# A decoder trunk layer in split float32 on one core: splits of the first projection in another order, operand sums and reloads elsewhere, square sums by single-column products

## The chip, the cores and the metric

The kernel runs on one core of a Trainium2 chip. The metric is the device time of one execution in microseconds. Three executions of the kernel before took 1136.26, 1137.62 and 1137.86 us (median 1137.62).

## The reference

One layer of a decoder trunk over 512 tokens of width 1024, all in float32:

```python
h = rms_norm(x, norm_mix)
rq, rk, rv, rg, cq, ckv, krope, gr, gm = split(h @ w_in)
ro = rms_norm(retention(rope(rq), rope(rk) * 256**-0.5, rv))        # 4 heads, 256 / 512 wide
a_ret = (ro * silu(rg)) @ w_br
q = rms_norm(rms_norm(cq) @ w_uq)                                   # 8 heads, 128 + 64 (rotary)
k_nope, v = split(rms_norm(ckv) @ w_ukv);  k = rms_norm([k_nope, krope])
a_mla = causal_attention(rope(q), rope(k), v) @ w_bm
x = x + (sigmoid(gr) * a_ret + sigmoid(gm) * a_mla) @ w_o
x = x + relu(rms_norm(x) @ w_up)**2 @ w_down                        # 4096 wide
x = x + sigmoid(rms_norm(x) @ w_ple_gate) * (p @ w_ple)
```

The norms of q and k in the attention need, for each head and token, the sum of squares over the 128 non-rotary channels (and the rotary ones): these are the square sums of this text.

## The kernel before

Activations lie with channels on the 128 partitions and the 512 tokens along the free axis, in [128, 512] tiles. Every float32 operand of a product is split into a high part of the matmul's reduced type and the remainder, and each product is three matmuls (`mm3`, line 168 in the profile: low times high, high times low, high times high), so nearly all TensorE work is matmuls of 512 columns. ScalarE writes the high part (`wh_...` of a weight chunk at line 261, `...h` of an activation in `split`), VectorE the rest (`wl_...` at line 263 or 265, `...l`). A product can start only when both are there.

The program is a list of steps (`step(key, function, arguments)`), run in order. A step with a weight key has its chunk of at most [128, 1024] fetched by SyncE's queue (`wr_...`) into one of six raw tiles and split one chunk ahead, into one of three pairs of split tiles, so a split of a chunk waits until TensorE is done with the chunk three earlier. TensorE's instructions keep the order of the list. Those of ScalarE, VectorE and POOL, and the transfers, are ordered by a scheduler where the code does not pin them (`keep_in_program_order`), and each engine then works its instructions off strictly in that order: one that waits holds all behind it.

Tiles of the working pool (`T`, 45 of them) and of a second pool for longer-lived operands (`K`, 16) are reused in turn; PSUM has eight banks (`B`).

The stages, with the names in the profile: the first projection `pA` (key-value latent; eight row chunks `a1`, operands `xg0` to `xg7` = x times a gain, 72 matmuls), the query latent `pcq`, the attention gates `gm` and the heads (`pk`, `pq`, `pv`, scores `sc`, transposes `pt`, output `mo`), with token statistics by matmuls against a column of ones (`stx`, `stkv`; each as two records of 128x1), then the attention branch `bm` with its gates `gb` reloaded from DRAM (`zm..d`), then four retention heads: `rq`, `rk`, the values `rv` for two heads at a time and the gate `rg`, both by Strassen-like products numbered 1, 7, 2, 6, 5, 4, 3 on sums of operand blocks (`x_operand`: s7, s6, s5, s3, each two tiles `..0` and `..1` with parts h and l), the masked scores `rs` (split into `ath` and `atl`, four blocks s.0 to s.3), the output `ro`, and the branch `br`. For the products 6 and 4 the weight blocks are summed in DRAM transfers that accumulate into the raw tile, issued by POOL. Branch sums and gates wait in DRAM and are reloaded (`re`, `ze`, `ge`, for the branch sum, the attention share and the retention gate), mixed (`mix`), and go through the output projection `wo`; then come the MLP (`up`, `dn`) and the gated embedding (`pg`).

The square sums of two heads (a pair) are formed in two steps: `pair_sums` sums squares with a [128, 32] block of ones, four products of 512 columns on four column groups of the array at once, ScalarE copies the result, and `pair_stats` turns four 128-token blocks with transposes (`st`), from which VectorE works out the head factors (`ha`, `hr`); these are broadcast (`pbk`) for the scores.

Before the first products, seven matmuls on a zeroed tile (`zero`) are issued. In the head of the program, three chunks and three operands are split in the order of the code's loop, the rest inside `first_products`.

## Time and profile before

| | |
|---|---|
| median of three executions | 1137.62 us (1136.26 to 1137.86) |
| the profiled execution | 1134.75 us |
| its span on the engines | 1133.0 us |
| mean granted TensorE clock | 0.993 |
| TensorE busy | 1108.0 us (98%), 5547 matmuls and as many weight loads |
| VectorE, ScalarE, POOL busy | 735.5, 537.1, 85.5 us |
| transfers | 175.97 MB, 155 GB/s over the span |

A row of a profile's list names line, engine, operation and output<-inputs, with buffer numbers left out (`wl_rk<-wr_rk,wh_rk`), then the count and times. The list of waits names the engine that stood, what it waited for, the sum, how often, and the longest. In the chain of waits each row is a stretch of the chain that ended last: start, length, what. A window row gives busy time with instruction counts for TensorE, its weight loads, VectorE, ScalarE and POOL, then the granted clock, the DMA share and GB/s.

### The profile page before, as it was taken

What the parts mean: (1) busy time and instruction counts of PE and PEld (TensorE: products, weight loads), DVE (VectorE), ACT (ScalarE), POOL (GpSimd) and SP (SyncE); (2) the same over time, 40 slices, a digit from 0 to 9 for tenths busy, and PEclk for the clock granted to TensorE, in tenths of its full rate; (3) what the DMA queues carried; (4) which work ended last, traced back from release to release, by engine and by line L of the source; (5) the groups of instructions that cost most, each with busy time, mean ns of one, the idle gap of its engine ahead of it and who ended that gap; (6) DMA issues with size and microseconds to landing.
All of it is one profiled execution on the core that took longest, in us unless ns stands there. A gap on an engine that the chain in (4) does not pass through costs nothing.

```text
span 1133.0 us, 14696 instructions
## 1 busy us (share of the span) xinstructions
PE 1108.0 (98%) x5547; PEld 938.7 (83%) x5547; DVE 735.5 (65%) x1206; ACT 537.1 (47%) x762; POOL 85.5 (8%) x113
## 2 busy tenths in 40 slices
PE   8999999999899999999999999999999999999998
PEld 6887878888689989888988977888888888888877
DVE  5787687565766755845684668646566566668675
ACT  6556656443354545444543543434444443445542
POOL 0000000001111011022003000010100100101000
PEclk8999999999899999999999999999999999999999
DMA  7223231356498265479638473694745855737511
GB/s 230 77 89 127 61 103 49 120 206 213 139 205 215 94 207 139 130 172 237 184 115 190 131 288 121 198 265 141 155 158 178 176 162 159 184 130 205 150 37 74
DMA packets 59223, 175.97 MB, mean 155 GB/s; under 512 B 7248, under 2 KB 8656, under 8 KB 58896
## 3 DMA queue, kind: packets, MB, share of 16 engines
q1 hardware_dynamic: 45168, 129.66, 33.6%
q0 software_dynamic: 13840, 45.36, 20.7%
q8 instruction: 43, 0.70, 0.2%
q14 instruction: 28, 0.23, 0.1%
q10 hardware_dynamic: 144, 0.03, 0.0%
HBM read 156.92 MB, written 15.99 MB: 153 GB/s over the span
## 4 chain that ended last, share of the span: by engine, by line
PE 90%; DVE 5%; DMA 2%; ACT 2%; issue 2%; SPq 0%; DVEq 0%; ACTq 0%
PE up L168 15%; PE dn L168 13%; PE rg L168 7%; PE rv L168 7%; PE br L168 6%; PE rk L168 4%; PE pg L168 4%; PE wo L168 3%; PE gr L168 3%; PE bm L168 3%; PE rq L168 3%; PE gm L168 3%; PE ro L168 3%; PE sc L168 2%; PE pA L168 2%
## 5 line engine op out<-in xcount | busy, mean ns | idle before, releaser
L168 PE MATMUL dn<-wh_dn,cl 128*128 128x512 f32 x224 | 87.2, 389 | 0.0
L168 PE MATMUL dn<-wh_dn,ch 128*128 128x512 f32 x224 | 87.2, 389 | 0.0
L168 PE MATMUL dn<-wl_dn,ch 128*128 128x512 f32 x224 | 87.1, 389 | 0.0
L261 ACT ACTIVATE wh_dn<-wr_dn 128x1024 fp32r<-128x1024 f32 x32 | 34.0, 1063 | 75.4 <-PE up L168 54.3
L261 ACT ACTIVATE wh_up<-wr_up 128x1024 fp32r<-128x1024 f32 x32 | 34.0, 1061 | 57.4 <-PE up L168 29.3
L263 DVE TENSOR_TENSOR wl_dn<-wr_dn,wh_dn 128x1024 fp32r<-128x1024 f32 x32 | 39.1, 1220 | 27.5 <-ACT wh_dn L261 27.5
L263 DVE TENSOR_TENSOR wl_up<-wr_up,wh_up 128x1024 fp32r<-128x1024 f32 x32 | 39.1, 1222 | 17.7 <-ACT wh_up L261 17.7
L263 DVE TENSOR_TENSOR wl_rg<-wr_rg,wh_rg 128x1024 fp32r<-128x1024 f32 x20 | 24.4, 1222 | 38.5 <-ACT wh_rg L261 38.3
L168 PEld LDWEIGHTS dn<-wh_dn,ch 128*128 128x128 f32 x224 | 42.0, 188 | 8.8
L168 PEld LDWEIGHTS dn<-wh_dn,cl 128*128 128x128 f32 x224 | 42.0, 188 | 8.8
L951 DVE SCALAR_TENSOR_TENSOR f<-up,bcx 128x512 f32<-128x512 f32 x32 | 20.6, 685 | 44.1 <-PE up L168 44.1
L168 PEld LDWEIGHTS dn<-wl_dn,ch 128*128 128x128 f32 x224 | 42.0, 188 | 8.6
L261 ACT ACTIVATE wh_dn<-dr_dn 128x1024 fp32r<-128x1024 f32 x24 | 25.5, 1060 | 42.2 <-PE up L168 29.1
L223 POOL DMA_DIRECT2D dr_dn<-wstream x24 | 21.4, 896 | 312.1 <-DVE rx L326 119.6
L263 DVE TENSOR_TENSOR wl_dn<-dr_dn,wh_dn 128x1024 fp32r<-128x1024 f32 x24 | 29.3, 1222 | 22.4 <-ACT wh_dn L261 22.4
L261 ACT ACTIVATE wh_rv<-wr_rv 128x1024 fp32r<-128x1024 f32 x28 | 29.6, 1059 | 28.5 <-PE rv L168 12.0
L261 ACT ACTIVATE wh_rg<-wr_rg 128x1024 fp32r<-128x1024 f32 x28 | 29.6, 1056 | 25.2 <-DMA wr_rg<-wstream 17.0
L263 DVE TENSOR_TENSOR wl_br<-wr_br,wh_br 128x1024 fp32r<-128x1024 f32 x16 | 19.6, 1222 | 24.4 <-ACT wh_br L261 20.2
L263 DVE TENSOR_TENSOR wl_rv<-wr_rv,wh_rv 128x1024 fp32r<-128x1024 f32 x20 | 24.5, 1224 | 15.9 <-ACT wh_rv L261 15.9
L1009 DVE TENSOR_TENSOR d<-d,dn 128x1024 f32<-128x1024 f32 x24 | 29.3, 1219 | 6.4 <-PE dn L168 6.4
L854 ACT ACTIVATE rt<-br 128x512 f32<-128x512 f32 x24 | 14.3, 597 | 36.1 <-PE br L168 32.3
L640 ACT ACTIVATE p<-p,ng,hr 128x128 f32<-128x128 f32 (+3 forms) x32 | 20.6, 646 | 15.6 <-DVE ng L638 15.5
(1820 smaller groups left out, 3619.9 us busy)
## 6 DMA issues: line engine op xcount, KB each, us to landing
wr_up<-wstream SPq DMA_DIRECT2D x32, 512.0 KB, 4.4
wr_dn<-wstream SPq DMA_DIRECT2D x32, 512.0 KB, 3.5
dr_dn<-wstream POOLq DMA_DIRECT2D x24, 512.0 KB, 7.5
wr_rv<-wstream SPq DMA_DIRECT2D x20, 512.0 KB, 4.1
wr_rg<-wstream SPq DMA_DIRECT2D x20, 512.0 KB, 4.7
wr_rv<-wstream POOLq DMA_DIRECT2D x16, 512.0 KB, 7.0
wr_rg<-wstream POOLq DMA_DIRECT2D x16, 512.0 KB, 5.7
wr_br<-wstream SPq DMA_DIRECT2D x16, 512.0 KB, 3.5
```

What stands on the lines that cost most here:

```text
L168: return tc.keep_in_program_order(nc.tensor.matmul(*a, **k))
L223: nc.gpsimd.dma_start(raw, chunk(("w", blk, kb, fb, c)), accum_op=ALU.add)
L261: ACT(hi, raw, AF.Copy, scale=sign)
L263: TT(lo, raw, hi.bitcast(F32), op=ALU.subtract)
L640: ACT(cols[b], cols[b], AF.Exp, bias=ng[:, b:b + 1], scale=d["rq"][:, b], accum_out=sums[:, b:b + 1])
L854: ACT(t, ps, AF.Copy)
L951: STT(u[:, i], ps[:, i], 0.0, V["bcx2"], op0=ALU.max, op1=ALU.mult)
L1009: TT(to, to, dps[p], op=ALU.add if sign > 0 else ALU.subtract)
```

## The change

Six edits:

1. The zero matmuls are nine, and come ahead of the loads; the splits of all eight operands and `a1` chunks stand in one loop ahead of the products, and ScalarE's high parts are pinned to that order. The two copies of the mask and identity (`maskr`, `identr`) are pinned too.
2. `pair_sums` is gone; `pair_stats` sums squares with 16 matmuls of one moving column (`stats`, as the token statistics do).
3. `x_operand` 7 is made after the fourth `bm` step instead of after the eighth, and 6, 5 and 3 among the first `rv` products; s7 lies in the working pool.
4. Two of four operands `rog` of the retention branch of heads 0 to 2, and
5. the reloads `re`, `ze`, `ge`, lie in the `K` pool instead of the working pool.
6. The first two tiles of `wo` are made in halves: k = 0 to 3 of both, then k = 4 to 7 of both.

```diff
-    for k in range(3):
+    for k in range(8):
+        if k >= 6:
+            prepare(("a1", k))
         load_chunk(("a1", k))
-        xg.append(split(xs[k], f"xg{k}", g(G_MIX + k)))
...
-    for i in range(7):
-        MM(ps, zero[:, 0:P], zero, start=i == 0, stop=i == 6)
+        xg.append(split(xs[k], f"xg{k}", g(G_MIX + k), pin=True))
...
-        if k >= 3:
-            xg.append(split(xs[k], f"xg{k}", g(G_MIX + k)))
...
-        ACT(maskr[:, P:2 * P], cst[:, C_MASK:C_MASK + P], AF.Copy)
-        ACT(identr, ident, AF.Copy)
+        tc.keep_in_program_order(ACT(maskr[:, P:2 * P], cst[:, C_MASK:C_MASK + P], AF.Copy))
+        tc.keep_in_program_order(ACT(identr, ident, AF.Copy))
...
-    def pair_sums(p):
-
-        ps = B(f"sums{p}")
+    def pair_stats(p):
+        st = blocks(B(f"st{p}"), 4)
         for i, (h, key) in enumerate(((2 * p, "sqk"), (2 * p + 1, "sqk"), (2 * p, "sqq"), (2 * p + 1, "sqq"))):
-            MM(ps[32 * i:32 * i + 32], ones, H[h][key], start=True, stop=True, tile_position=(0, 32 * i),
-               skip_group_check=True)
-        V["sums", p] = T(f"sums{p}")
-        ACT(V["sums", p], ps, AF.Copy)
-
-    def pair_stats(p):
-        sums, ps = V["sums", p], B(f"st{p}")
-        for b in range(4):
-            MM(ps[:, b * P:b * P + P], sums[:, b * P:b * P + P], ident, is_transpose=True, start=b == 0, stop=b == 3,
-               skip_group_check=True)
-        st = ps.rearrange("p (b c r) -> p b c r", b=4, r=32)[:, :, :, 0]
+            stats(st[:, :, i:i + 1], H[h][key], first=i == 0, last=i == 3)
...
-            hl = split(t, None, hi=K(f"s{p}{c}h", F32R), lo=K(f"s{p}{c}l", F32R))
+            new = T if p == 7 else K
+            hl = split(t, None, hi=new(f"s{p}{c}h", F32R), lo=new(f"s{p}{c}l", F32R))
...
-            d["rog"][m] = split(d["og"][m], f"rog{h}{m}")
+            new = K if m < 2 and h < RH - 1 else T
+            d["rog"][m] = split(d["og"][m], None, hi=new(f"rog{h}{m}h", F32R), lo=new(f"rog{h}{m}l", F32R))
...
-            t = T(f"{nm}{n}")
+            t = K(f"{nm}{n}")
             nc.sync.dma_start(t, l[n])
...
+    def out_part(w, n, part):
+        if part == 0:
+            wo_ps[n] = B(f"wo{n}")
+        for k in range(4 * part, 4 * part + 4):
+            mm3(wo_ps[n], cut(w, k * P), mixed[k], k == 0, k == 7)
...
+        if n == 3:
+            step(None, x_operand, 7)
-    for p in (1, 7, 2, 6, 5, 4, 3):
+    for p in (1, 2, 4):
         step(None, x_operand, p)
...
+            if h == 0 and p in (1, 7, 2):
+                step(None, x_operand, {1: 6, 7: 5, 2: 3}[p])
...
+    for n in range(2):
+        step(("o", n), out_part, n, 0)
     for n in range(8):
         step(("o", n), out_proj, n)
```

The scheduler orders the engines anew around these edits. Three places matter later. The first is the start of ScalarE's program; `wh_a_k` is the high part of weight chunk k, `xgkh` that of operand k, and the rows at line 385 square x. Before:

```order
L261 ACTIVATE wh_a_0_119<-wr_a_0_89 128x384
L261 ACTIVATE wh_a_1_127<-wr_a_1_93 128x384
L261 ACTIVATE wh_a_2_135<-wr_a_2_97 128x384
L307 ACTIVATE xg0h<-x_88,gn 128x512
L307 ACTIVATE xg1h<-x_92,gn 128x512
L307 ACTIVATE xg2h<-x_96,gn 128x512
L385 ACTIVATE x_88<-x_88 128x512
```

and with the change:

```order
L261 ACTIVATE wh_a_0_131<-wr_a_0_101 128x384
L309 ACTIVATE xg0h<-x_100,gn 128x512
L261 ACTIVATE wh_a_1_139<-wr_a_1_105 128x384
L309 ACTIVATE xg1h<-x_104,gn 128x512
L261 ACTIVATE wh_a_2_147<-wr_a_2_109 128x384
L309 ACTIVATE xg2h<-x_108,gn 128x512
L389 ACTIVATE x_100<-x_100 128x512
L389 ACTIVATE x_104<-x_104 128x512
```

The operand of k = 0 moved from behind the third chunk's split to behind the first chunk's.

The second is VectorE shortly before the first `rk` product. `wl_rk_0` is the low part of its weight; `s50l` to `s31l` are the low parts of operand sums, at line 724 of before the sums themselves. Before:

```order
L724 TENSOR_TENSOR sx_2973<-xr_2804,sx_2973 128x256
L305 TENSOR_TENSOR s51l<-sy_3006,s51h 128x512
L724 TENSOR_TENSOR sx_2974<-xr_2848,sx_2974 128x256
L305 TENSOR_TENSOR s30l<-sx_2973,s30h 128x512
L724 TENSOR_TENSOR sx_2974<-xr_2892,sx_2974 128x256
L769 TENSOR_TENSOR rqb_3057<-rq_3031,trs 128x512
L263 TENSOR_TENSOR wl_rk_0_3063<-wr_rk_0_3060,wh_rk_0_3062 128x1024
```

and with the change, `xn7l` being the last normalised operand and `gb<-gb,bm` a product with a reloaded gate:

```order
L679 TENSOR_TENSOR gb_2897<-gb_2897,bm_2899 128x512
L692 SCALAR_TENSOR_TENSOR xr_2928<-xr_2928,gn,rbc 128x512
L265 TENSOR_TENSOR wl_rk_0_3047<-wr_rk_0_3044,wh_rk_0_3046 128x1024
L307 TENSOR_TENSOR xn7l<-xr_2928,xn7h 128x512
L713 TENSOR_TENSOR sx_2834<-xr_2928,sx_2834 128x256
L307 TENSOR_TENSOR s61l<-sx_2834,s61h 128x512
```

The weight's low part left the end of the operand sums and stands now right behind the gate product of bm5, ahead of the last two gate products.

The third is VectorE in the third retention head (h = 2). The rows are the masking of scores `s<-rs,dec`, the low parts `atl<-s` of the four score blocks (512, 384, 256 and 256 wide), the gate sum `z` and the low part `wl_rg` of the accumulated weight chunk of product 4. Before:

```order
L789 TENSOR_TENSOR s_5345<-rs_5338,dec_5314 128x256
L789 TENSOR_TENSOR s_5356<-rs_5349,dec_5314 128x256
L305 TENSOR_TENSOR atl<-s_5334,ath 128x384
L305 TENSOR_TENSOR atl<-s_5345,ath 128x256
L305 TENSOR_TENSOR atl<-s_5356,ath 128x256
L741 TENSOR_TENSOR z_11_5278<-z_11_5278,rg_5365 128x512
L265 SCALAR_TENSOR_TENSOR wl_rg_5498<-wr_rg_5207,wh_rg_5497 128x1024
```

and with the change:

```order
L307 TENSOR_TENSOR atl<-s_5345,ath 128x512
L307 TENSOR_TENSOR atl<-s_5356,ath 128x384
L307 TENSOR_TENSOR atl<-s_5367,ath 128x256
L784 TENSOR_TENSOR s_5378<-rs_5371,dec_5336 128x256
L736 TENSOR_TENSOR z_11_5300<-z_11_5300,rg_5387 128x512
L267 SCALAR_TENSOR_TENSOR wl_rg_5520<-wr_rg_5229,wh_rg_5519 128x1024
L307 TENSOR_TENSOR atl<-s_5378,ath 128x256
```

The low part of the fourth block (the second row of 256 behind the 384 before, the last row of the changed piece) moved behind the weight's; ScalarE's high parts, and the same rows of the first head (h = 0), moved alike.

## The prediction

> **What bounds the kernel now.** I read the page first (TensorE is busy 98% of the span), then the waits of TensorE, which list every place where it stood still.

> ```profile
> PE rk L168 <- DVE wl_rk L263: 5.7, 1, 5.7
> PE pA L168 <- ACT xg0h L307: 4.2, 1, 4.2
> PE br L168 <- ACT rog30h L304: 2.1, 1, 2.1
> PE zero L168 <- DVE zero L369: 1.5, 1, 1.5
> PE pt3a L168 <- DVE p L643: 1.3, 1, 1.3
> PE pg L168 <- ACT bcx L936: 1.2, 1, 1.2
> PE pbk L168 <- DVE hr L601: 0.8, 1, 0.8
> PE sc L168 <- ACT sqk L524: 0.8, 1, 0.8
> PE sqr L168 <- DVE mx L634: 0.8, 1, 0.8
> PE pt0a L168 <- DVE p L643: 0.7, 1, 0.7
> PE wo L168 <- DVE mix7l L305: 0.6, 1, 0.6
> PE wo L168 <- ACT mix7h L304: 0.4, 1, 0.4
> PE br L168 <- DVE rog30l L305: 0.4, 1, 0.4
> ```

> Nothing else in 1133.0 us waits noticeably. A change can therefore gain only by closing one of these waits or by taking work off TensorE, and it loses whatever it adds to TensorE. Two of the waits cost more than their length, as the view by windows shows (columns: busy time of each engine, then the granted clock and the DMA share).

> ```profile
> 9.00:15.30 6.30, 6.30 (x14) 4.69 (x15) 4.68 (x7) 5.08 (x11) 0.00 (x0) 0.50 1.04 390
> ...
> 313.00:352.00 39.00, 38.99 (x174) 31.89 (x173) 26.46 (x31) 22.39 (x28) 6.01 (x7) 1.00 0.93 221
> ```

> and of TensorE alone:

> ```profile
> 298.60:305.50 6.90, 5.92 (x14) 0.51 0.36 101
> ```

> Behind each of the two long waits TensorE runs 14 matmuls at half clock. The chain of waits says what that costs:

> ```profile
> 9.00 19.76 PE pA L168 x72
> ...
> 34.20 0.79 PE stx L168 x8
> ...
> 41.20 1.77 PE stkv L168 x16
> ...
> 78.59 1.00 PE sums L168 x8
> ...
> 299.58 13.90 PE rk L168 x48
> ...
> 395.93 10.88 PE rk L168 x48
> ```

> At full clock 48 matmuls of 512 columns take 10.88 us, 0.2267 us each; the first rk group takes 13.90, so 3.02 us are lost to the clock there. The 72 products of the first projection should take 72 x 0.2267 = 16.3 us and take 19.76.

> **The change, part by part** (minus is faster; the sum is made against the profiled execution's own 1134.75 us).

> *First projection.* The start is set by ScalarE, which takes its instructions in order.

> ```profile
> 7.81 0.52 ACT L261 ACTIVATE wh_a<-wr_a 128x384 fp32r<-128x384 f32 x1 [1.69 <-DMA wr_a<-wstream]
> 8.24 0.71 ACT L307 ACTIVATE xg0h<-x,gn 128x512 fp32r<-128x512 f32 x1
> ```

> xg0h stands behind the third chunk's split, which waits for its DMA until 7.81. In the changed order it is ScalarE's second instruction, behind wh_a_0 alone. What it then waits for is x0:

> ```profile
> 1.18 0.42 SPq L360 DMA_DIRECT2D x<-xT  x1
> ```

> and, in the list of transfers of the first 3 us, the time to landing:

> ```profile
> x<-xT SPq DMA_DIRECT2D x2, 256.0 KB, 3.8
> ```

> 1.18 + 3.8 = 5.0 us, plus 0.71 for xg0h: the products begin at about 5.7 instead of 9.00, a gain of 3.3. The nine zero matmuls (two more) end at about the same moment, so there is no idle stretch in front, and the half-clock stretch of 9 to 15.3 should go: 14 matmuls in 6.30 us instead of 14 x 0.2267 = 3.17, another 3.1. Not all of the 6.4 can be kept: at full clock the products of one k take 2.04 us, ScalarE and VectorE need 0.5 + 0.7 us and more for each k with the squares between, and the third chunk still lands at 7.8. With a stall of some 0.8 us before k = 1 and 2 I take -5.6; the ends are -6.4 and -3.3 (clock still half). [...] The two mask copies that wait behind later work on ScalarE I put at +0.2 (a little more at sqr, 0 to 0.4).

> *Square sums.* Four times TensorE loses the sums (1.00 us, row above) and their four transposes:

> ```profile
> 82.42 0.60 PE L168 MATMUL st<-cst,sums 128*128 128x128 f32 x4
> 82.77 0.48 PE L168 MATMUL gm<-xg0h,wl_gm 128*128 128x512 f32 x1
> ```

> (82.77 - 82.42 = 0.35), and gains 16 matmuls with one moving column. The nearest row is stx: four such matmuls, 8 records, 0.79 us on the chain. Sixteen, at 0.11 a record as the 16 records of the key statistics (stkv, 1.77) do too, are 3.54 us. Per pair 3.54 - 1.35 = +2.19, four pairs +8.8. It is TensorE's own time, so nothing hides it, except where TensorE stood waiting in the same stretch for ScalarE or VectorE (pt3a 1.3, sc 0.8, sqr 0.8). Walking the waits pair by pair I get about +2.0, +2.9, +1.4, +2.2: +8.5, with +6.5 (all those stalls partly filled) and +10 as ends. [...]

> *Operand sums and the rk wait.* VectorE holds the weight split for which rk waits:

> ```profile
> 288.71 0.69 DVE L686 TENSOR_TENSOR gb<-gb,bm 128x512 f32<-128x512 f32 x1 [3.11 <-ACT gb L685]
> ...
> 298.31 1.21 DVE L263 TENSOR_TENSOR wl_rk<-wr_rk,wh_rk 128x1024 fp32r<-128x1024 f32 x1
> ```

> ```profile
> 283.13 1.06 ACT L261 ACTIVATE wh_rk<-wr_rk 128x1024 fp32r<-128x1024 f32 x1 [1.20 <-PE bm L168]
> ```

> wh_rk is ready at 284.2, but wl_rk comes at 298.31, behind a 3.1 us wait for a gate reload and 9.6 us in which fifteen operand instructions of 0.4 to 0.7 us run. In the new order wl_rk_0_0 stands ahead of both reload products, so it ends at about 285.5, and rk starts right behind rq, at 299.58 - 5.66 = 293.9. Without the idle stretch the clock should not drop: -5.66 - 3.02 = -8.7. The moved instructions are the same ones; operand 7 is now made beside the bm products, the others beside rv, where VectorE is idle a third of the time (26.46 of 39.00, the window 313 to 352 above); cover gone, each would delay rv by its 0.7 us, and I count none. wl_rk_0_1 is now behind the two reloads; it is needed 5.44 us into rk, at 299.2, and even a reload that lands 5 us later (two weight chunks have moved ahead of it in SyncE's queue) leaves it at about 296. Ends: -8.7, and 0 if that margin is gone and the clock falls again.

> *Retention heads 0 and 2.* The new order moves something here too: on ScalarE wh_rg040 and wh_rg240 now come ahead of the fourth score split (ath<-s03, ath<-s23), and on VectorE wl_rg040 and wl_rg240 ahead of atl<-s03, atl<-s23. Those chunks come by an accumulating POOL transfer that is issued late.

> ```profile
> 555.36 0.86 POOL L223 DMA_DIRECT2D wr_rg<-wstream  x1 [10.20 <-DVE wl_rg L263]
> ```

> ```profile
> wr_rg<-wstream POOLq DMA_DIRECT2D x16, 512.0 KB, 5.7
> ```

> ```profile
> 558.52 0.40 PE L168 MATMUL ro<-ath,rv1110l 128*128 128x512 f32 x1
> ```

> ```profile
> 561.80 1.23 DVE L265 SCALAR_TENSOR_TENSOR wl_rg<-wr_rg,wh_rg 128x1024 fp32r<-128x1024 f32 x1 [1.52 <-ACT wh_rg L261]
> ```

> The first ro product reaches the fourth block after 3 x (512 + 384 + 256) columns, 1.53 us, at 560.05. The split of that block now follows wl_rg240: 561.80 + 1.23 + 0.4 = 563.4. That is a new wait of 3.3 us. Queued behind it on TensorE is all of ro, and behind ro the rest of the gate. In head 0 the same sum is milder:

> ```profile
> 367.15 0.40 PE L168 MATMUL ro<-ath,rv0110l 128*128 128x512 f32 x1
> ```

> ```profile
> 368.26 1.23 DVE L265 SCALAR_TENSOR_TENSOR wl_rg<-wr_rg,wh_rg 128x1024 fp32r<-128x1024 f32 x1 [1.56 <-ACT wh_rg L261]
> ```

> 369.9 against 367.15 + 1.53 = 368.7: 1.1 us. Together +4.4; the ends are 0 (the transfers land 3 us sooner in the shifted program) and +5. Heads 1 and 3 keep their order.

> *Reloads and the last branch.*

> ```profile
> 669.41 1.06 ACT L261 ACTIVATE wh_br<-wr_br 128x1024 fp32r<-128x1024 f32 x1 [2.23 <-PE gr L168]
> ...
> 670.85 0.62 ACT L304 ACTIVATE rog30h<-og 128x512 fp32r<-128x512 f32 x1
> ```

> rog30h waits on ScalarE behind the sigmoids of the reloads and behind a weight split that waits for gr. With the reloads in the kept tiles, issued from head 3 on, rog30h to rog33h come before wh_br_3_1, and br starts without its 2.1 + 0.4 us: -2.4 (0 if the sigmoids still come late). The last reloads now stand behind wr_o on SyncE and wait for tiles that the first mixes free while br runs (96 x 0.2267 = 21.8 us, to about 691); only mix5 to mix7 at its end use them, so I count nothing.

> *Output halves.* The first halves of wo0 and wo1 need mix0 to mix3 only; the 24 matmuls between (5.4 us) cover the mix7 waits of 0.4 + 0.6: -0.9.

> Sum: -5.6 + 0.2 + 8.5 - 8.7 + 4.4 - 2.4 - 0.9 = -4.5, so 1130.25 for a run like the profiled one. The median of the runs shown, 1137.62, lies 2.87 above that execution; I keep the difference: **1133.1 us**.

> **The rivals.** (A) *No retention wait*: all as above, but the accumulated chunks come early enough. For it: the wait is the latency of one transfer each, some 5.7 us, and nothing else. Against it: the POOL transfer is released by VectorE's preceding split, which has not moved. -8.9, 1128.7. (B) *The attention turns the other way, slower*: the 3.5 us of statistics now stand directly ahead of the factor chain st, hr, pbk instead of several microseconds earlier, so TensorE waits for hr in every pair. For it: pbk already waits 0.8 once. Against it: other products are queued between. If each of the four pairs loses the full price of the new stretch once more (2.2 us), +8.8: 1141.9. It decides the sign from 4 x 1.7 us on. (C) *The rk wait only moves*: wl_rk_0_1 or the first rv split is late by some 2 us and the clock drops for a window (3.0). For it: the reload that stops VectorE is now later in SyncE's queue; against it: the 3 us margin above. -8.7 becomes about -4: 1137.8. [...]

> **How the numbers follow.** Forecast 0.46, A 0.20, B 0.13, C 0.17, D 0.04. A change under 0.2%, 2.3 us, can't be told from none, so faster means below 1135.3. The forecast, A and D are there, with a little of C: 0.70. Same: most of C and the forecast's edge, 0.16. Slower: B and the rest of C, 0.14. The range takes in A, most of D and the forecast with its bounds, and C: 1126 to 1139; B and the far end are left out.

> **What would show it.** pA begins below 6 us with clock 1.0 and ends near 23; rk is no longer in the list of waits and its group takes 10.9; a chain entry st of 3.5 us stands in each of four pairs; ro waits for atl in heads 0 and 2 by about 1 and 3 us; br and wo are gone from the list. It would be wrong if a stretch of half clock remains at 9 or 299 us, if pbk waits 2 us in each pair, or if ro does not wait.

## The result, and the profile after

The changed kernel is slower. Its median over 18 executions is 1141.89 us (1138.15 to 1152.15), that of the kernel before, over as many, 1136.44 (1134.5 to 1138.42); the ratio is 1.0056, with a 95% interval from 1.0036 to 1.0076. The forecast was 1133.1, faster, in a range of 1126 to 1139. The profiled execution took 1140.53 us, its span is 1138.8, and its mean granted clock 0.989 where it had been 0.993. Not only the median is new: the executions of the changed kernel lie 14 us apart, those of before 4.

The list of TensorE's waits has become shorter, as it should. It begins so:

```profile
PE pbk L168 <- DVE hr L594: 2.7, 2, 2.5
PE zero L168 <- DVE zero L361: 1.5, 1, 1.5
PE ro L168 <- DVE atl L307: 1.3, 2, 0.9
PE st L168 <- DVE mx L627: 1.3, 1, 1.3
PE pg L168 <- ACT bcx L944: 1.2, 1, 1.2
...
PE wo L168 <- DVE wl_o L265: 0.6, 1, 0.6
...
PE ro L168 <- ACT ath L306: 0.3, 1, 0.3
```

rk, pA at its long wait, and br are gone. What is lost is not in this list. It stands in the windows of the attention, from the first query latent to the first bm product, before (first row) and after (second; us, TensorE's busy time, granted clock, DMA share, GB/s):

```profile
28.60:239.40 210.80, 206.26 (x1142) 1.00 0.30 94
```

```profile
23.80:254.80 231.00, 225.32 (x1221) 0.95 0.28 86
```

The stage took 210.8 us at full clock and takes 231.0 at 0.95 of it: 20.2 us more. TensorE's idle time in it grew by only 1.1 us, from 4.5 to 5.7. Seven windows of 3.41 us in it ran at half clock; before there was none in this stage. The seven lie on one grid of 3.41 us: they begin at 39.15, 117.66, 127.90, 162.03, 165.45, 168.86 and 206.41. The windows around the statistics of the four pairs show where they come from (TensorE alone):

```profile
80.11:83.53 3.42, 3.42 (x24) 1.00 0.61 186
114.25:117.66 3.41, 3.41 (x27) 1.00 0.03 5
117.66:121.07 3.41, 3.41 (x10) 0.50 0.26 77
124.49:127.90 3.41, 0.89 (x7) 1.00 0.18 65
127.90:131.31 3.41, 3.41 (x19) 0.50 0.31 91
...
162.03:172.27 10.24, 10.24 (x38) 0.50 0.41 106
202.99:206.41 3.42, 3.42 (x27) 1.00 0.22 77
206.41:209.82 3.41, 3.41 (x10) 0.50 0.00 0
```

and the part of the square sums (`st`) in such windows:

```profile
76.70:80.11 3.41, 1.74 (x17) 1.00 0.49 154
80.11:83.53 3.42, 1.88 (x17) 1.00 0.61 186
114.25:117.66 3.41, 2.43 (x22) 1.00 0.03 5
117.66:121.07 3.41, 0.00 (x0) 0.50 0.26 77
...
202.99:206.41 3.42, 2.44 (x22) 1.00 0.22 77
```

In the window from 114.25 TensorE never stood still, and yet the next window has half the clock. 2.43 us of it were single-column matmuls, 2.44 in the one from 202.99. Where the statistics fell evenly across two windows, 1.74 and 1.88 us, the clock stayed. The window from 127.90 follows one in which TensorE stood 2.5 us for pbk. So six of the seven stand at the second to fourth pair, one of them behind the wait for pbk. The seventh is not due to the new square sums:

```profile
35.74:39.15 3.41, 3.41 (x25) 1.00 0.00 0
39.15:42.57 3.42, 3.42 (x10) 0.50 0.24 77
```

The first of these windows holds the 16 records of `stkv` (1.93 us busy), which both kernels have, and four 128-column matmuls (0.5 us) beside them. Before, the same run lay across the end of a window and nothing followed; here it falls into one.

In the chain of waits the third pair takes longest, since its own matmuls run at the lowered clock:

```profile
78.53 3.46 PE st L168 x32
...
113.22 3.46 PE st L168 x32
...
161.04 6.06 PE st L168 x32
...
309.37 10.88 PE rk L168 x48
```

The last row answers to the 13.90 us of before: rk now takes its 10.88.

Stage by stage, from the starts of the stages in the two profiled executions (changed minus before, what each stage added):

| stage | predicted | measured |
|---|---|---|
| to the first query latent (pA) | -5.6 | -4.8 |
| attention (square sums; mask copies) | +8.5; +0.2 | +20.2 |
| rq, rk and up to rv | -8.7 | -8.7 |
| retention heads, up to the last branch | +4.4 | +2.8 |
| last branch, br | -2.4 | -2.3, and -0.8 within it |
| output projection, wo | -0.9 | -0.6 |
| sum | -4.5 | +5.8 |

The sum is the difference of the spans, 1138.8 - 1133.0. Every row but that of the attention is within 1.6 us of its term.

### The profile page after: what moved, and what is told of

Read it like the earlier page. It is cut to its first block, busy times and chain, and to the rows that moved or that the text cites. A ratio compares the mean times of both kernels' runs of the same rounds, so it can differ in the third digit from the quotient of the medians.

```text
span 1138.8 us, 14873 instructions
## 1 busy us (share of the span) xinstructions
PE 1123.0 (99%) x5629; PEld 956.7 (84%) x5629; DVE 734.7 (65%) x1206; ACT 535.2 (47%) x758; POOL 85.7 (8%) x113
## 4 chain that ended last, share of the span: by engine, by line
PE 88%; DMA 4%; DVE 4%; ACT 2%; issue 2%; SPq 0%; ACTq 0%; DVEq 0%; POOLq 0%
PE up L168 15%; PE dn L168 13%; PE br L168 6%; PE rg L168 5%; PE rv L168 5%; PE pg L168 4%; PE rq L168 4%; PE rk L168 4%; PE bm L168 4%; PE gm L168 4%; PE wo L168 4%; PE gr L168 4%; DMA wr_rg<-wstream 3%; PE ro L168 2%; PE sc L168 2%
## 5 line engine op out<-in xcount | busy, mean ns | idle before, releaser
L168 PE MATMUL dn<-wh_dn,cl 128*128 128x512 f32 x224 | 87.2, 389 | 0.0
L168 PE MATMUL dn<-wh_dn,ch 128*128 128x512 f32 x224 | 87.2, 389 | 0.0
L168 PE MATMUL dn<-wl_dn,ch 128*128 128x512 f32 x224 | 87.1, 389 | 0.0
L261 ACT ACTIVATE wh_dn<-wr_dn 128x1024 fp32r<-128x1024 f32 x32 | 34.0, 1062 | 75.3 <-PE up L168 54.3
L261 ACT ACTIVATE wh_up<-wr_up 128x1024 fp32r<-128x1024 f32 x32 | 34.0, 1061 | 57.3 <-PE up L168 29.3
L265 DVE TENSOR_TENSOR wl_dn<-wr_dn,wh_dn 128x1024 fp32r<-128x1024 f32 x32 | 39.0, 1220 | 26.6 <-ACT wh_dn L261 26.6
L265 DVE TENSOR_TENSOR wl_up<-wr_up,wh_up 128x1024 fp32r<-128x1024 f32 x32 | 39.1, 1222 | 17.7 <-ACT wh_up L261 17.6
L265 DVE TENSOR_TENSOR wl_rg<-wr_rg,wh_rg 128x1024 fp32r<-128x1024 f32 x20 | 24.3, 1224 | 39.0 <-ACT wh_rg L261 38.6
L168 PEld LDWEIGHTS dn<-wh_dn,cl 128*128 128x128 f32 x224 | 42.1, 188 | 8.8
L168 PEld LDWEIGHTS dn<-wh_dn,ch 128*128 128x128 f32 x224 | 42.1, 188 | 8.7
L168 PEld LDWEIGHTS dn<-wl_dn,ch 128*128 128x128 f32 x224 | 42.1, 188 | 8.6
L261 ACT ACTIVATE wh_dn<-dr_dn 128x1024 fp32r<-128x1024 f32 x24 | 25.4, 1060 | 43.2 <-PE up L168 29.1
L223 POOL DMA_DIRECT2D dr_dn<-wstream x24 | 21.8, 908 | 304.0 <-DVE wl_dn L265 119.1
L265 DVE TENSOR_TENSOR wl_dn<-dr_dn,wh_dn 128x1024 fp32r<-128x1024 f32 x24 | 29.4, 1223 | 23.2 <-ACT wh_dn L261 23.2
L261 ACT ACTIVATE wh_rv<-wr_rv 128x1024 fp32r<-128x1024 f32 x28 | 29.6, 1059 | 29.0 <-PE rv L168 12.0
L261 ACT ACTIVATE wh_rg<-wr_rg 128x1024 fp32r<-128x1024 f32 x28 | 29.3, 1055 | 24.2 <-DMA wr_rg<-wstream 18.9
L265 DVE TENSOR_TENSOR wl_br<-wr_br,wh_br 128x1024 fp32r<-128x1024 f32 x16 | 19.5, 1220 | 21.6 <-ACT wh_br L261 21.6
L265 DVE TENSOR_TENSOR wl_rv<-wr_rv,wh_rv 128x1024 fp32r<-128x1024 f32 x20 | 24.4, 1223 | 13.7 <-ACT wh_rv L261 13.7
## 6 DMA issues: line engine op xcount, KB each, us to landing
wr_up<-wstream SPq DMA_DIRECT2D x32, 512.0 KB, 4.2
wr_dn<-wstream SPq DMA_DIRECT2D x32, 512.0 KB, 3.5
dr_dn<-wstream POOLq DMA_DIRECT2D x24, 512.0 KB, 7.8
wr_rv<-wstream SPq DMA_DIRECT2D x20, 512.0 KB, 3.8
wr_rg<-wstream SPq DMA_DIRECT2D x20, 512.0 KB, 4.6
wr_rv<-wstream POOLq DMA_DIRECT2D x16, 512.0 KB, 6.6
wr_rg<-wstream POOLq DMA_DIRECT2D x16, 512.0 KB, 6.7
wr_br<-wstream SPq DMA_DIRECT2D x16, 512.0 KB, 3.6
```

Of the source, the lines that this page charges most:

```text
L168: return tc.keep_in_program_order(nc.tensor.matmul(*a, **k))
L223: nc.gpsimd.dma_start(raw, chunk(("w", blk, kb, fb, c)), accum_op=ALU.add)
L261: i = ACT(hi, raw, AF.Copy, scale=sign)
L265: TT(lo, raw, hi.bitcast(F32), op=ALU.subtract)
```

## The experiments

The theory after the result (clock): a stretch of single-column matmuls does not count as work for the clock; a window of 3.41 us with too much of it is followed by one at half clock, which costs 1.7 us, half of 3.41. The rival: the loss comes from waits and from the price of the products, and lowered clocks only follow standstill. The kernel before was run again beside each set; its median there was 1134.8, 1134.8 and 1134.1, where it had been 1136.4 beside the changed kernel. So kernels of different sets are compared by their distance from the kernel before beside them: the changed kernel's is +5.5.

### The old square sums back

```diff
 # in the changed kernel
+    step(None, pair_sums, 0)                      # and for each later pair, as before
-            stats(st[:, :, i:i + 1], H[h][key], first=i == 0, last=i == 3)
+            MM(ps[32 * i:32 * i + 32], ones, H[h][key], ..., tile_position=(0, 32 * i))   # copy, four transposes
```

> The changed kernel with one part undone: the square sums of a pair are again four products of 512 columns on four column groups, a copy and four transposes. Theory (clock): the changed kernel gains 14 to 15 us outside the attention and loses 20.2 us in it, of which 8.5 are the products themselves and about 12 are seven windows of 3.41 us at half clock. With the sums back the attention costs what it did: the span falls from 1138.8 by about 20 to 1118 to 1120, the median to about 1121 to 1123, faster than both kernels, with no half-clock window between 75 and 250 us. Rival (the loss comes from the new order of ScalarE and VectorE in the attention, which the pinned splits of the start and the moved operand sums bring, the statistics being only its 8.5 us): a gain of about 9 us, median near 1132, with waits of pbk and the half-clock windows still there.

Measured: 1122.15 us (1119.93 to 1127.61), ratio 0.9899 (0.9877 to 0.9921). The attention is back at 210.8 us without a half-clock window:

```profile
23.70:234.50 210.80, 206.27 (x1141) 1.00 0.30 94
```

The kernel is 12.6 us faster than before; that is what the rest of the change was worth. Against the changed kernel's +5.5, one part of six cost 18 us in the medians, and 20.2 in the attention of the profiles. The spread within this kernel is still 8 us. The profiled execution is one of its two longest (1127.19), and its waits show where:

```profile
PE ro L168 <- ACT ath L306: 2.3, 2, 1.7
PE ro L168 <- DVE atl L307: 1.8, 2, 0.9
```

```profile
354.92:358.33 3.41, 1.90 (x11) 1.00 0.18 31
358.33:361.74 3.41, 3.41 (x14) 0.50 0.73 251
549.48:552.89 3.41, 1.38 (x8) 1.00 0.38 145
552.89:559.72 6.83, 6.21 (x20) 0.50 0.44 156
```

The waits of ro are the predicted ones of heads 0 and 2 (4.1 us in sum), and a window in which they leave TensorE 1.4 to 1.9 us of work is followed by half clock.

### The new square sums alone

```diff
 # in the kernel before
-    step(None, pair_sums, 0)                      # and for each later pair
-        (products against 32 columns, copy, transposes)
+            stats(st[:, :, i:i + 1], H[h][key], first=i == 0, last=i == 3)
```

> The kernel before with one part of the change alone: the square sums by 16 matmuls of one moving column. Theory (clock): 8.5 us of products plus four to seven half-clock windows at 1.7 us each, so 15 to 20 us slower than before, near 1153, and spread by several us from run to run, since it hangs on where the windows fall. Rival (statistics cost only their products): 8 to 9 us slower, near 1145, spread as before.

Measured: 1154.79 us (1151.22 to 1157.07), 20.0 us slower than before, ratio 1.0166 (1.015 to 1.0183). The attention:

```profile
28.10:260.80 232.70, 227.02 (x1221) 0.94 0.28 85
```

21.9 us more than 210.8. Eight windows at half clock, all of them at the four pairs, 8 x 1.7 = 13.6, and 8.4 of products (3.46 instead of 1.35 us a pair) make 22.0; with 1.1 us more of idle time the sum is 1.2 too high, so 1.7 for a window is a little too much. The rival's 8 to 9 us is out.

### The new square sums, set apart

```diff
 # in the changed kernel: four groups of four matmuls a pair, wide matmuls between them
+    for i in range(3):
+        fill(1)
+        step(None, pair_part, 0, i)
...
+                step(None, pair_part, p + 1, 0)
                 step(("v", p + 1), value_pair, p + 1)
+                step(None, pair_part, p + 1, 1)
...
+                step(None, pair_part, p + 1, 2)
+                fill(1)
                 step(None, pair_stats, p + 1)      # the fourth group, then the factors
```

> The changed kernel with the same 16 single-column matmuls for each pair, but set apart in four groups of four (0.9 us each) with 12 to 24 wide matmuls between them; nothing else is left out. Theory (clock): a window holds 0.9 us, at most 1.8 us, of narrow work, no half-clock window follows, and the time is that of the kernel with the old sums plus 8.8 us, 1129 to 1132: about 10 us faster than the changed kernel. Rival (price of the products and waits of the factor chain): the same number of products costs the same, 1139 to 1143.

Measured: 1137.6 us (1133.4 to 1145.3), ratio 1.0032 (1.0016 to 1.0048). This fits neither number: it is 2.8 us slower than before, so 2.6 better than the changed kernel, where the theory said about 10. The attention takes 226.3 us instead of 231.0:

```profile
23.70:250.00 226.30, 219.57 (x1222) 0.98 0.30 94
```

Three windows at half clock are left in it. One, at 88.61, follows a standstill of 2.1 us for pbk in the first pair. One, at 160.29, follows a window with 1.5 us of standstill and 0.8 us of single-column matmuls; it holds 1.70 us of them itself, and the window behind it has half the clock too. The waits:

```profile
PE pbk L168 <- DVE hr L599: 2.6, 2, 2.1
...
PE mo L168 <- DVE mx L632: 1.5, 1, 1.5
```

So narrow work alone never lowered a full clock here, but the edit also moved filler matmuls, and TensorE now stands still in the first pair for pbk and before mo, where the changed kernel did not. As a test of the clock it was not clean; the next one is.

### Bursts as a probe

```diff
 # in the kernel before
+    def burst(n, m):
+        st = blocks(B(f"burst{n}"), 1)
+        for i in range(m):
+            MM(st[:, i % 4], ident, ones[:, 0:1], start=i == 0, stop=i == m - 1, skip_group_check=True)
...
         step(("bm", n), branch_m, n)
+        step(None, burst, n, (4, 6, 7, 8, 9, 10, 12, 16)[n])     # behind wo: the same backwards
```

> A probe on the kernel before: behind each of the eight tiles of bm and of wo (24 wide matmuls, 5.4 us each) stands one burst of single-column matmuls that nobody reads, 4, 6, 7, 8, 9, 10, 12 and 16 long behind bm and the same backwards behind wo; at 0.22 us each they last 0.9 to 3.5 us. No work is left out. Theory (clock): a window of 3.41 us that a burst covers so far that only about a third of the wide matmuls is left (5 of 16) is followed by a window at half clock, one with 7 or more is not; so the bursts of 4 to 7 never lower the clock, those of 12 and 16 nearly always do, those between by where the window falls. Rival (a matmul of any width counts as work, and the half-clock windows of the attention come from standing still): no half-clock window at any burst, and the kernel longer by 2 x 72 x 0.22 = 32 us and no more.

Measured (one execution): 1167.67 us. Five bursts of the sixteen are followed by a half-clock window. First the share of the bursts in two windows, then TensorE in the windows behind them:

```profile
262.12:265.53 3.41, 1.80 (x16) 1.00 0.65 229
733.16:736.57 3.41, 2.16 (x20) 1.00 0.56 132
```

```profile
265.53:268.95 3.42, 3.42 (x16) 1.00 0.45 141
736.57:739.99 3.42, 3.42 (x10) 0.50 0.60 180
```

1.80 us of narrow work in a window left the clock at 1.00 (16 matmuls in the next), 2.16 halved it (10). The other four windows that did held 2.7 to 3.4 us, all others 1.8 or less. In two of these four, at 286.02 and 296.26, TensorE was busy for the whole 3.41 us; the first:

```profile
286.02:289.43 3.41, 3.41 (x29) 1.00 0.90 150
289.43:292.84 3.41, 3.41 (x10) 0.50 0.60 195
```

The rival, that any matmul counts as work, is out, though its time was near: the kernel is 32.9 us slower than before, by accident, since the bursts take 144 x 0.22 = 31.7, the five half-clock windows come on top, and rk waits 0.5 us instead of 5.7. In the changed kernel 1.88 us of single-column matmuls in a window of 3.41 without idle time left the clock at 1.00, so the limit lies between that and the 2.16 here. The rest of the two windows is 1.54 and 1.25 us; that wide matmuls must fill about two fifths of a window is an estimate from these.

### The retention order

```diff
 # the fourth score block's split, and product 4's accumulated chunk, in the order of the code
+            if j == 3:
+                tc.keep_in_program_order(i)        # ath <- s.3
+                tc.keep_in_program_order(k)        # atl <- s.3
...
+        if late:                                   # the chunk of rg, product 4
+            tc.keep_in_program_order(i)            # wh, and wl below
```

With the old sums:

> The kernel with the old sums, and in the retention the splits of the fourth score block and of the accumulated weight chunk of product 4 pinned to the order in which the code has them, so that the score block is split first. The waits of ro for atl (1.3 and 0.3 us in the changed kernel's list) should go: 1 to 2 us faster than the kernel with the old sums alone. Rival: the weight chunk is split so much later that rg waits instead by as much or more: no gain, or 1 to 2 us slower.

Measured: 1117.84 us (1117.65 to 1119.18), ratio 0.9853 (0.9841 to 0.9866): 4.3 us faster than without the pins, more than expected, and the best of all. No wait of ro is left, no window at half clock behind the start (clock 1.0), and the four executions agree within 1.5 us. Its waits begin:

```profile
PE zero L168 <- DVE zero L364: 1.5, 1, 1.5
PE pt3a L168 <- DVE p L650: 1.3, 1, 1.3
PE pg L168 <- ACT bcx L962: 1.2, 1, 1.2
```

With the new sums:

> The changed kernel, statistics and all, with only the retention's fourth score block pinned ahead of the accumulated weight chunk. If the retention wait is worth the same 4.3 us with the statistics as without them: 1136 to 1139, still with the wide spread, since the half-clock windows of the attention stay. If the pinned order only paid because it met the old sums: no difference to the changed kernel, 1140 to 1143.

Measured: 1137.76 us (1133.13 to 1141.68), 3.0 us slower than before, so 2.5 better than the changed kernel, still spread over 8 us. With this spread the medians alone decide little: the ratios' intervals overlap (1.0011 to 1.0044, and 1.0036 to 1.0076). The profiles are clearer. From the first rv product to the last product ahead of the last br they show 355.7 us before, 358.4 in the changed kernel and 355.7 here: the pins take back the whole loss of 2.8 us with the new sums too.

### The start alone

```diff
 # in the kernel before: nine zero matmuls first, the splits of all k in one loop, pinned
-    for k in range(3):
+    for k in range(8):
...
+        xg.append(split(xs[k], f"xg{k}", g(G_MIX + k), pin=True))
```

> The kernel before with the start alone as in the change (nine zero matmuls first, the splits in the loop's order, the mask copies pinned). The traces give 4.8 us until pcq; if all is kept to the end, 4 to 5.5 us faster, near 1130. If the attention gives it back, because its waits stand at other places of the clock's windows, 2 us or less.

Measured: 1132.01 us, ratio 0.9967 (0.9952 to 0.9982): 2.8 us. In the profile bm begins 5.3 us earlier, but the rk wait has grown:

```profile
PE rk L168 <- DVE wl_rk L263: 5.7, 1, 5.7
```

```profile
PE rk L168 <- DVE wl_rk L265: 8.0, 1, 8.0
```

(before, and with the start alone). The first rv product is 4.1 us earlier, so 1.2 are given back there, and 1.6 more in the last branch. There TensorE stands still for `rog30h` and `rog30l` as long as before (2.1 + 0.4 us), but before this lay across two windows, and with the start alone it falls into one:

```profile
667.22:670.64 3.42, 2.15 (x10) 1.00 1.05 414
670.64:674.05 3.41, 2.18 (x8) 1.00 1.01 390
```

```profile
665.21:668.63 3.42, 0.92 (x4) 1.00 1.05 419
668.63:672.04 3.41, 3.41 (x10) 0.50 0.55 205
```

Beside the moved operand sums and pools, which take both waits away, more of the gain is kept: with the pins, the kernel with the old sums is 16.9 us faster than before, the one with only the operand sums and pools (below) 12.2. The 4.7 between them are the start and the wo halves (0.6).

### The operand sums alone, with room, and with the pins

```diff
 # in the kernel before
+        if n == 3:
+            step(None, x_operand, 7)              # s7 in the working pool
-    for p in (1, 7, 2, 6, 5, 4, 3):
+    for p in (1, 2, 4):
...
+            if h == 0 and p in (1, 7, 2):
+                step(None, x_operand, {1: 6, 7: 5, 2: 3}[p])
```

> The kernel before with the operand sums alone moved as in the change. The rk wait and its half-clock windows go (8.7 us), and the new order of the fourth score block and the accumulated weight chunk comes in with it, since this edit alone moves those instructions: 4 us lost again by waits of ro and windows at half clock. Net 4 to 5 us faster, near 1130.5. If the retention wait hangs on the other edits instead: 8 to 9 us faster, near 1126.

Measured: 1143.11 us (1139.26 to 1146.72), ratio 1.0069 (1.0043 to 1.0096): 8.3 us slower, where 4 to 5 faster was expected. rv of the first heads starts 9.6 us earlier, 8.7 of it from rq and rk, as it should. From there to the last branch it loses 16.4 us, most of it at the second rv stage and in the last head:

```profile
PE rv L168 <- ACT cv L737: 4.2, 2, 4.1
...
PE so L168 <- DVE sqo L805: 2.8, 1, 2.8
```

cv stands on ScalarE for 3.70 us until the transfer of a branch sum to DRAM (`ret5d<-rt`) is done, and a branch sum's copy before it 6.05 for the one before that. That suggested a lack of working tiles: operand 7 keeps four of the 45. The next kernel adds the two pool edits of the change:

```diff
+            new = K if m < 2 and h < RH - 1 else T           # rog
...
-            t = T(f"{nm}{n}")
+            t = K(f"{nm}{n}")                                # re, ze, ge
```

> The kernel before with the moved operand sums and with the reloads and half of rog in the K pool; start, square sums and wo as before. If the operand sums alone were slow because operand 7 takes four of the 45 working tiles and ScalarE then waits for tiles (rv for cv 4.1 us, so for sqo 2.8 us, with half-clock windows behind them), the K pool gives those tiles back: both waits go, the rk gain of 8.7 and the br gain of 2.5 us show, less about 4 us for the retention order: 1126 to 1129. If the second rv stage is late for another reason: those waits stay, 1140 or more.

Measured: 1125.53 us (1124.16 to 1127.37), ratio 0.9922 (0.9907 to 0.9936). The waits of rv and so are gone; those of ro remain:

```profile
...
PE ro L168 <- ACT ath L304: 1.2, 1, 1.2
PE ro L168 <- DVE atl L305: 0.9, 1, 0.9
```

> The same with the retention's fourth score block pinned ahead of the accumulated weight chunk: no wait of ro, no half-clock window there, 4 us less, 1122 to 1124. Rival: the pinned order gains only beside the changed start; then as without it.

Measured: 1121.96 us (1121.75 to 1122.58), ratio 0.989 (0.9874 to 0.9907): 3.6 us from the pins. The waits came out as expected, and the times lie 0.5 and 0.04 us below their ranges. Which of the two pool edits gave the room was not tested. The pool edits alone were not tried, because operand 7 stands in the K pool until the operand edit takes it out.

## Why the prediction was wrong

**Square sums: this step failed.** The term was +8.5, "TensorE's own time", and the products did cost that: 4 x (3.46 - 1.35) = 8.4. Left out was what they do to the clock. Six half-clock windows at the pairs cost up to 6 x 1.7 = 10.2 us, and 1.1 are added idle time. The seventh window, behind `stkv`, came from where the grid of windows fell. Together this is 21.4 against 20.2 measured, so 1.7 a window is a little too much here as well. The step treated the two half-clock stretches of before as an effect of standing still, since that is what the two rows showed. The trace of before could not have shown the limit: its longest run of single-column matmuls, the 1.77 us of `stkv`, lay across the end of a window, 1.55 us in one and 0.38 in the next. But the term could have been asked from the other side: is a stretch of 3.5 us, as long as a window, with almost no columns moved, work or idleness for the clock? The runs answer it: the clock fell after windows of 3.41 us without any idle time, with 2.43 and 2.44 us of narrow work in them. That the spread comes from where the windows fall in each execution is the author's estimate, since one execution of each kernel was traced; shown is the granted clock, 0.992 in the execution of 1138.30 us and 0.982 in that of 1152.15.

**Rival B** had the sign and, by accident, the time (1141.9), not the cause: pbk waits 2.5 us in one pair, not in four. The 0.04 of D stood for a lower price of a record, and no run shows one: 32 records in 3.46 us are 0.108 each, no cheaper than the 8 of `stx` in 0.79.

**Start.** -5.6 forecast, -4.8 measured, but part of that is chance. In the six profiles with the old start the first query latent begins at 27.1 to 28.6 us, and before's is the latest; in the six with the new start it begins at 23.3 to 23.9. The gain by these is 3.2 to 5.3. Alone, 2.8 us of it reach the end. The prediction added this term and that of rk as if independent.

**rk.** -8.7 forecast, -8.7 measured; the margin of wl_rk_0_1 was there, and rival C did not occur.

**Retention.** +4.4 forecast (its own rows, 3.4 and 1.2, give 4.6), +2.8 measured in the profiled execution, of which 1.6 are the waits of ro for atl and ath. The wait was forecast mainly in head 2 (3.3, and 1.1 in head 0); the changed kernel's profile has it the other way round, ro taking 0.6 us longer in head 2 and 1.7 in head 0. In the medians of one set the pins that remove it are worth 4.3 and 3.6. The reason given, a split queued behind an accumulated chunk, holds: with the block pinned ahead the waits are gone in all three kernels, and the stage is back within 0.2 us of before. The size varies with the clock: in the profile of the kernel with the old sums back, where half-clock windows follow the waits, the stage lost 9.8 us.

**Reloads, br, wo.** -2.4 and -0.9 forecast; -2.3 and -0.6 measured, with 0.8 more inside br. wo still waits once, 0.6 for wl_o. The prediction has no term for operand 7's four tiles in the working pool. That did no harm only because the K pool took half of rog and the reloads at the same time: without them the operand edit is 8.3 us slower than before, with them 8.6 faster.

## What to carry to other kernels

Ask of each stretch on TensorE not only how long it is but how much of a clock window it leaves to wide matmuls: here single-column sums of more than about 2 us in 3.41 cost up to another 1.7 us for each window at half clock, and a spread from run to run came with it (14 us, before 4). Short waits can cost more than their length in the same way where several lie in one window: the last branch's 2.5 us did with the start alone, where they fell into one window and 1.6 us more were lost, and did not in the kernel before, where they lay across two. Gains that end at the same wait do not add: test edits together and with one undone, since here the parts that were tried alone (+20.0, -2.8, +8.3) say nothing of the whole (+5.5).

## What the runs showed of the hardware

Idle time lowered the clock by the same windows: 2.5 us in one did (124.49 to 127.90 in the changed kernel), 1.3 and 1.2 in two neighbours did not (667.22 to 674.05 before). Near 1.5 us both occurred: 1.51 did (354.92 to 358.33 with the old sums back), 1.54 did not in the kernel with the new sums alone (689.73 to 693.14).

The standstill of 4.2 us before pA was followed by matmuls 0.43 us apart, where they later are 0.23, until 15.3 us before, until 12.4 in the kernel with operand sums and pools and until 12.9 in the same with the pins. In the last the profile has no record of the clock before 12.89, and its windows show 1.00 there: at the start the clock has to be read from the distance of the matmuls.
